# Sixteen merge projections of a hybrid layer: pairs of block products with weight sums and a hand-made order

## The chip, the cores and the metric

The kernel runs on one core of a Trainium2 chip. A core has TensorE (PE, matrix products; its weight loads appear as PEld), VectorE (DVE), ScalarE (ACT), GpSimd (POOL) and SyncE (SP, which issues most DMAs). The metric is device time in microseconds (us), median of several runs. One execution is also profiled; its times are those of the profile's rows.

## What is computed

One layer over 640 tokens (128 of a prompt, 512 of a sample) of width 1024, in fp32. A long convolution branch and a neighbourhood attention branch each give a gated 1024-wide result (here yh and ya). What matters for the change is how they are merged:

```python
p_h = (y_h * silu(g_h)) @ w_bh          # yh . w_bh
p_a = (y_a * silu(g_a)) @ w_ba          # ya . w_ba
m_h, m_a = split(sigmoid(m), 2)         # m: a projection of the layer's input h
out = (m_h * p_h + m_a * p_a) @ w_out
x_new = layer_norm(ALPHA * x + gate * out)
```

## The kernel before

Everything is kept transposed: 128 channels of a tile on the partitions, 640 tokens along the free axis, so 1024 channels are eight tiles (NK = 8). A product of fp32 accuracy is made of three passes in a faster 32-bit format: a value x is split into a high part xh (ACT copies it into that format) and a low part xl = x - xh (DVE), and x.w is taken as wh.xh + wh.xl + wl.xh. `split` (L97) does this; `wtile` (L130) loads a 128x1024 weight tile into a `raw` buffer (two of them) on SP's queue and splits it into `wh` and `wl`. With `eng == "dma"` ACT writes -w instead and a GpSimd DMA (L143) adds the weight onto it.

`proj` (L171) is one projection: an output tile of 128 channels by 640 tokens in a two-bank PSUM tile, by `accumulate` (L161): for each of 8 k tiles three passes of two matmuls of 320 tokens, 48 matmuls. In the profile all of them have the line L166.

The stages are: prologue, convolution, attention (until about 682 us), then the merge:

- `mix_a(n)` (L979) projects h for the gate of the attention branch, tanh on ACT. Two of them come first. The gates of the convolution branch (`mix_h`, L932) were projected during attention.
- The loop at L990: for each n of 8, `proj(T_BH + n, yhH, yhL)`: yh . w_bh. yh is split into yhH (eight 640-token tiles) and yhL. L993 multiplies the result by the gate. Beside it ya is split (yaH, yaL), and `next(side)` runs one of eight gate calls (`gate_rows` L970, `ada` L231: a weight `gate` into a raw buffer, 16 small matmuls).
- The loop at L1018: for each n `mix_a(n + 2)`, then `proj(T_BA + n, yaH, yaL)`: ya . w_ba, gate (L1023), addition of the convolution branch's part (L1024), split into mH and mL, which reuse the tiles of yhH and yhL. After the fifth `gate_bias` (L1002) makes gbc, the gate row of the last addition, by broadcast matmuls.
- L1036: the eight out weights are loaded and split into buffers that are free by then (the tiles of hH and hL among them, which hold h until the last mix_a).
- `out_tile` (L1052) makes one of five out tiles (128 tokens by 1024) of 48 matmuls of 512, `norm_tile` (L1073) gates it, adds x and normalizes, on DVE.

In this stage the order on each engine comes from a scheduler, as far as the waits allow; in the attention PE's order is written by hand.

Of the kernel before, what the change touches and what calls it, by code (L numbers as in the profile page):

```python
# [15 lines left out]
D = 1024  # L16
LP = 128
LS = 512
NK = 8
# [26 lines left out]
def tile_hyena_natten_step(ctx: ExitStack, tc: tile.TileContext, a, o):  # L46
# [57 lines left out]

    out = {"yh": {}}

    def load_pack(i):
# [10 lines left out]

    hH = hp.tile([P, NK, NT], F32R, tag="hH", name="hH")
    hL = hp.tile([P, NK, NT], F32R, tag="hL", name="hL")  # L120
    st = const.tile([P, NK, 32], F32, tag="st", name="st")
# [48 lines left out]

    def proj(i, xh=None, xl=None, eng=None):  # L171
        if i in banks:
            return banks.pop(i)
        w = wtile(i, eng)
        ps = bank(i)
        for k in range(NK):
            accumulate(ps, w, k, xh[k] if xh else hH[:, k], xl[k] if xl else hL[:, k])
            if k < NK - 1:
                yield
        return ps  # L180
# [60 lines left out]
    def prologue():  # L241
# [7 lines left out]
        def work(items, ps):  # L249
            for item in items.split():  # L250
                if item[0] == "w":
                    for _ in range(int(item[1:])):
                        nc.tensor.matmul(ps[:, 256:], hid[:, :P], hid[:, :256], start=True, stop=True, skip_group_check=True)  # L253
                else:
                    i, j = int(item[0]), int(item[1])
                    accumulate(banks[i], early[i], j, hH[:, j], hL[:, j], lead=(0, 1, 2) if j < 1 else (0, 2, 1))

# [18 lines left out]
        for k in range(NK):  # L276
# [32 lines left out]
            for c, s0, n in ((0, PC, LP), (1, SC, LS)):  # L309
                cs = slice(s0, s0 + n)  # L310
                nc.vector.tensor_scalar(hx[:, cs], xt[:, cs], mod[:, 1, c : c + 1], mod[:, 0, c : c + 1], op0=ALU.mult, op1=ALU.add)
                nc.scalar.activation(hH[:, k, cs], xt[:, cs], AF.Identity, scale=mod[:, 1, c : c + 1], bias=mod[:, 0, c : c + 1])  # L312
            nc.vector.tensor_tensor(hL[:, k], hx[:], f(hH[:, k]), op=ALU.subtract)  # L313
            if k == 0:
# [336 lines left out]
    yh, ident = out["yh"], out["ident"]  # L651

# [53 lines left out]
    def values(m):  # L706
# [5 lines left out]
        def passes(k):  # L712
            wh, wl = w[k // 4][0][k % 4], w[k // 4][1][k % 4]
            return ((hH, wh, k == 0, False), (hL, wh, False, False), (hH, wl, False, k == NK - 1))

        for half in range(2):
            ks = range(4 * half, 4 * half + 4)
            for k in ks:
                for x, wk, first, last in passes(k):
                    for t in range(4):  # L720
                        nc.tensor.matmul(  # L721
                            ps[:, t // 2, t % 2 * 256 : t % 2 * 256 + 256], x[:, k, P * t : P * t + P], wk,
                            start=first and t % 2 == 0, stop=last, skip_group_check=True,
                        )
                yield
            if half:
                nc.scalar.activation(v[:, :1024], ps[:].rearrange("p a b -> p (a b)"), AF.Copy)
            else:
                pe = ps_mm.tile([P, 2, 512], F32, tag="mm", name=f"ve{m}")[:, 0]
            for k in ks:  # L730
                for x, wk, first, last in passes(k):
                    nc.tensor.matmul(pe[:, :256], x[:, k, P * 4 :], wk, start=first, stop=last, skip_group_check=True)  # L732
            yield
# [14 lines left out]

    tail = ctx.enter_context(ExitStack())
    ac = ctx.enter_context(ExitStack())  # L750
    ya, tms, edges, biases = [], [], {}, {}

    def attention_setup():
        nonlocal at, mask
        hy.close()
        yap = out["yap"] = tail.enter_context(tc.tile_pool(name="yap", bufs=1, side="right"))
        ya.extend(row(yap, "ya", f"ya{j}", bufs=NK) for j in range(NK))
        at = ac.enter_context(tc.tile_pool(name="at", bufs=1, side="right"))
# [107 lines left out]

    def gated(j, cols, o_):
        nc.vector.tensor_tensor(ya[j][:, cols], out[f"sg{j}"][:, cols], o_, op=ALU.mult)

# [17 lines left out]
    def tiled(i):  # L887
# [39 lines left out]
    def gate_a(j):  # L927
        out[f"sg{j}"] = sg = at.tile([P, NT], F32, tag="sg", bufs=2, name=f"sg{j}") if j else row(yhp, "yh", "sg0")
        yield from gate_tile(T_GA + j, sg[:])
        yield  # L930

    def mix_h():  # L932
        homes = ((0, "q"), (0, "k"), (0, "v"), (), (0, "ql"), (0, "kl"), (1, "q"), (1, "ql"))
        for n in range(NK):
            th = slot(*homes[n], f"mh{n}") if homes[n] else th
            th, pair = (pair[:, NT:], None) if n == 3 else (th[:, :NT], th)
            ps = (yield from proj(T_MH + n))[2]
            nc.scalar.activation(two(th), ps[:, :, :HALF], AF.Tanh, scale=0.5)
            out[f"mh{n}"] = th
            yield  # L940
# [20 lines left out]

    mp = tail.enter_context(tc.tile_pool(name="mp", bufs=1, side="right"))
    lp = left.enter_context(tc.tile_pool(name="lp", bufs=1))
    gpart = slot(1, "v", "gpart")[:, :D]
    yhH = [row(lp, "yhH", f"yhH{n}", F32R, NK) for n in range(NK)]
    yhL = []
    yaH = [row(mp, "yaH", f"yaH{n}", F32R, NK) for n in range(NK)]
    yaL = []

# [9 lines left out]
    def mix_a(n):  # L979
        ps = now(proj(T_MA + n))[2]  # L980
        th = mp.tile([P, NT], F32, tag="th", bufs=3, name=f"mta{n}")
        nc.scalar.activation(two(th[:]), ps[:, :, :HALF], AF.Tanh, scale=0.5)
        return th

    side = gate_rows()
    mtas = [mix_a(0), mix_a(1)]
    for n in range(NK):
        yhL.append(row(yhp, "yh", f"yhL{n}", F32R))
        split(yhH[n][:], yhL[n][:], yh[n][:])
    for n in range(NK):  # L990
        th = out[f"mh{n}"]
        ps = now(proj(T_BH + n, yhH, yhL))[2]
        nc.vector.scalar_tensor_tensor(two(th), two(th), 1.0, ps[:, :, :HALF], op0=ALU.add, op1=ALU.mult)  # L993
        yaL.append(row(out["yap"], "ya", f"yaL{n}", F32R, NK)[:] if n else slot(1, "kl", "yaL0", F32R)[:, :NT])
        split(yaH[n][:], yaL[n], ya[n][:])
        next(side, None)
    mH, mL = yhH, yhL
    gbc = lp.tile([P, 2, D], F32, tag="gbc", name="gbc")
    eps = lp.tile([P, 1], F32, tag="eps", name="eps")
    nc.gpsimd.memset(eps[:], LN_EPS)  # L1000

    def gate_bias():  # L1002
        selr = lp.tile([P, 2], F32R, tag="selr", name="selr")
# [3 lines left out]
        gt = out["slots_r"].tile([P, 2, 384], F32R, tag="k", name="gt")  # L1007
        for c0, n in ((0, 384), (384, 384), (768, 256)):
# [8 lines left out]

    for n in range(NK):  # L1018
        th = mtas.pop(0)
        if n + 2 < NK:  # L1020
            mtas.append(mix_a(n + 2))
        ps = now(proj(T_BA + n, yaH, yaL))[2]
        nc.vector.scalar_tensor_tensor(two(th[:]), two(th[:]), 1.0, ps[:, :, :HALF], op0=ALU.add, op1=ALU.mult)  # L1023
        nc.vector.tensor_tensor(th[:], th[:], out[f"mh{n}"], op=ALU.add)  # L1024
        split(mH[n][:], mL[n][:], th[:])
        next(side, None)
        if n == 4:
            gate_bias()

    wo = []  # L1030
    woh = lp.tile([P, D], F32R, tag="woh", name="woh")
    wol = wp.tile([P, D], F32R, tag="wl", bufs=3, name="wol0")
    wohH = hp.tile([P, 5, D], F32R, tag="hH", name="wohH")
    wolH = hp.tile([P, 5, D], F32R, tag="hL", name="wolH")
    for k in range(NK):
        raw = wp.tile([P, D], F32, tag="raw", name=f"wo{k}")  # L1036
        load_to(raw[:], a["wall"][T_WO + k])
        if k == 0:
            wo.append((woh[:], wol[:]))
        elif k < 6:  # L1040
            wo.append((wohH[:, k - 1], wolH[:, k - 1]))
        else:
            wh = wp.tile([P, D], F32R, tag="wh", name=f"woh{k}")
            wl = wp.tile([P, D], F32R, tag="wl", bufs=3, name=f"wol{k}")
            wo.append((wh[:], wl[:]))
        split(*wo[k], raw[:])


    tail.close()
    fin = ctx.enter_context(tc.tile_pool(name="fin", bufs=1, side="right"))  # L1050
    bc = fin.tile([P, 2, D], F32, tag="bc", name="bc")
    def out_tile(t, split_cols):  # L1052
# [188 lines left out]
```

## Time and profile before

| | |
|---|---|
| median of 3 runs | 925.84 us (925.32 to 926.7) |
| the profiled run | 925.7 us |
| its span | 923.9 us |
| merge and out projection | from about 682 us on |
| last matmul | ends at 915.6 us |
| DVE, ACT, POOL busy | 53%, 41%, 16% of the span |

In a row of a group stand: line, engine, operation, output <- inputs, shape, count; then busy time in all and mean ns of one; then the idle time of its engine just ahead of it and what ended that. A row of the DMA list has the size of one transfer and the median time from issue to landing. A row of the chain of waits in order of time has start, length, engine, line and count of the instructions in that piece.

### The profile page before, as it was taken

The page shows a single profiled execution, that of the slowest core. Times are in us where ns is not written, and L with a number is a line of the kernel's source. Part 1 is how long each engine was busy: PE and PEld are TensorE (multiplying, and loading weights), DVE is VectorE, ACT ScalarE, POOL GpSimd, SP SyncE. Part 2 cuts the span into 40 slices and gives each one's busy share as a digit, 9 for nine tenths or more (in the row PEclk, how much of TensorE's full clock was granted, in tenths as well). Part 3 has the DMA queues.
Part 4 walks back from the last instruction along what each step waited for, and adds up shares of the span by engine and source line. Part 5 has one row for each costly group of instructions (what it writes and reads, how often), then busy time and mean ns, then how long its engine had stood idle before and what let it go on. Part 6 is the DMA issues. An engine that isn't in the chain of part 4 may idle for free.

```text
span 923.9 us, 16758 instructions
## 1 busy us (share of the span) xinstructions
PE 910.2 (99%) x6856; PEld 877.4 (95%) x6856; DVE 486.4 (53%) x948; ACT 380.4 (41%) x776; POOL 146.2 (16%) x188
## 2 busy tenths in 40 slices
PE   8999999999999999999999999999999999999996
PEld 7899999999999999999999999999999999999885
DVE  4776775693796676445352533432261223335676
ACT  4485455554545334255454544444261112223200
POOL 0011010110010000474454543331000000000000
PEclk9999999999999999999999999999999999999998
DMA  8966664655465113242222221212123343224631
GB/s 320 380 161 135 128 149 98 137 133 123 100 141 126 50 49 85 86 122 67 71 68 69 67 70 58 72 49 70 48 69 113 120 146 99 72 69 116 205 114 69
DMA packets 36553, 102.13 MB, mean 111 GB/s; under 512 B 4316, under 2 KB 13020, under 8 KB 36477
## 3 DMA queue, kind: packets, MB, share of 16 engines
q1 hardware_dynamic: 32300, 86.35, 28.9%
q0 software_dynamic: 4032, 14.68, 9.8%
q8 instruction: 54, 0.88, 0.4%
q14 instruction: 23, 0.18, 0.1%
q10 hardware_dynamic: 144, 0.03, 0.0%
HBM read 97.38 MB, written 3.67 MB: 109 GB/s over the span
## 4 chain that ended last, share of the span: by engine, by line
PE 95%; DVE 2%; ACT 2%; issue 1%; POOL 0%; POOLq 0%
PE mm L166 65%; PE out L1065 6%; PE v L721 5%; PE s L788 2%; PE s L831 2%; PE pt L824 2%; PE ve L732 1%; PE adaT L236 1%; PE adaT L253 1%; PE yb L151 1%; PE yb L153 1%; PE yb L152 1%; PE gate L236 0%; PE fl L384 0%; PE fl L385 0%
## 5 line engine op out<-in xcount | busy, mean ns | idle before, releaser
L166 PE MATMUL mm<-hH,wh 128*128 128x320 f32 x1120 | 263.3, 313 | 0.9 <-ACT hH L312 0.6
L166 PE MATMUL mm<-hH,wl 128*128 128x320 f32 x1120 | 259.7, 310 | 0.4 <-DVE wl L99 0.4
L166 PE MATMUL mm<-hL,wh 128*128 128x320 f32 x1120 | 259.1, 310 | 0.0
L99 DVE TENSOR_TENSOR wl<-raw,wh 128x1024 fp32r<-128x1024 f32 x66 | 81.6, 1237 | 231.9 <-ACT wh L98 231.7
L166 PEld LDWEIGHTS mm<-hH,wh 128*128 128x128 f32 x1120 | 186.7, 188 | 6.2 <-issue 4.2
L166 PEld LDWEIGHTS mm<-hH,wl 128*128 128x128 f32 x1120 | 188.0, 188 | 1.4 <-DVE wl L99 1.1
L166 PEld LDWEIGHTS mm<-hL,wh 128*128 128x128 f32 x1120 | 188.2, 188 | 1.1 <-DVE hL L313 0.5
L98 ACT ACTIVATE wh<-raw 128x1024 fp32r<-128x1024 f32 x66 | 69.8, 1059 | 216.8 <-PE mm L166 95.9
L143 POOL DMA_DIRECT2D wl<-wall x28 | 24.3, 869 | 264.0 <-ACT wl L142 208.8
L144 ACT ACTIVATE wh<-raw 128x1024 fp32r<-128x1024 f32 x28 | 29.7, 1060 | 42.9 <-PE mm L166 42.7
L808 POOL TENSOR_SCALAR p<-p,sm 128x384 f32<-128x384 f32 x32 | 42.1, 1326 | 27.7 <-DVE sm L807 27.7
L1095 POOL TENSOR_TENSOR r<-r,bc 128x64 f32<-128x64 f32 x1 | 0.3, 320 | 249.7 <-ACT r L1094 249.7
L808 POOL TENSOR_SCALAR edge<-edge,sm 128x320 f32<-128x320 f32 x32 | 35.5, 1121 | 0.0
L474 DVE SCALAR_TENSOR_TENSOR x<-zs,pack,x 128x641 f32<-128x641 f32 x32 | 28.3, 884 | 12.1 <-ACT x L472 12.0
L826 ACT ACTIVATE pts<-pt 128x384 f32<-128x384 f32 x64 | 26.2, 502 | 11.0 <-PE pt L824 11.0
L142 ACT ACTIVATE wl<-raw 128x1024 fp32r<-128x1024 f32 x28 | 30.0, 1071 | 0.0
L166 PE MATMUL mm<-yhH,wh 128*128 128x320 f32 x128 | 29.9, 315 | 0.0
L166 PE MATMUL mm<-yaH,wh 128*128 128x320 f32 x128 | 29.2, 309 | 0.0
L166 PE MATMUL mm<-yhL,wh 128*128 128x320 f32 x128 | 29.2, 309 | 0.0
L166 PE MATMUL mm<-yaH,wl 128*128 128x320 f32 x128 | 29.2, 309 | 0.0
L166 PE MATMUL mm<-yaL,wh 128*128 128x320 f32 x128 | 29.2, 309 | 0.0
L166 PE MATMUL mm<-yhH,wl 128*128 128x320 f32 x128 | 29.2, 309 | 0.0
(330 smaller groups left out, 1677.7 us busy)
## 6 DMA issues: line engine op xcount, KB each, us to landing
raw<-wall SPq DMA_DIRECT2D x96, 512.0 KB, 3.6
wl<-wall POOLq DMA_DIRECT2D x28, 512.0 KB, 5.8
ada<-wada SPq DMA_DIRECT2D x16, 512.0 KB, 8.1
gate<-wada SPq DMA_DIRECT2D x8, 512.0 KB, 3.7
wo<-wall SPq DMA_DIRECT2D x8, 512.0 KB, 3.7
xt<-xT SPq DMA_DIRECT2D x8, 320.0 KB, 8.1
dec<-decay SPq DMA_DIRECT2D x20, 128.0 KB, 3.5
x<-xB SPq DMA_DIRECT2D x5, 512.0 KB, 3.8
```

Of the source, the lines that this page charges most:

```text
L98: hi = nc.scalar.activation(dst_h, src, AF.Copy)
L99: return hi, (eng or nc.vector).tensor_tensor(dst_l, src, f(dst_h), op=ALU.subtract)
L142: nc.scalar.activation(wl, raw[:], AF.Copy, scale=-1.0)
L143: nc.gpsimd.dma_start(wl, a["wall"][i], accum_op=ALU.add)
L144: nc.scalar.activation(wh, raw[:], AF.Copy)
L166: nc.tensor.matmul(ps[hf][:, :HALF], wt[k], x[:, hf * HALF : (hf + 1) * HALF], start=(i == 0 and k == 0), stop=(i == lead[2] and k == NK - ...
L474: nc.vector.scalar_tensor_tensor(d, zs[:, c : c + NG], convw[:, i, c : c + 1], d, op0=ALU.mult, op1=ALU.add)
L721: nc.tensor.matmul(ps[:, t // 2, t % 2 * 256 : t % 2 * 256 + 256], x[:, k, P * t : P * t + P], wk, start=first and t % 2 == 0, stop=last, ...
L788: nc.tensor.matmul(dst[h], x[rows(h), qs], y[rows(h), ks], start=i == 0, stop=i == 2, skip_group_check=True)
L808: nc.gpsimd.tensor_scalar_mul(pv, pv, sm[:, 2:3])
L826: nc.scalar.activation(ptS[:], pt[:, :384], AF.Copy)
L1065: ins = nc.tensor.matmul(dst, m[k][:, c0 : c0 + P], w[:, c : c + n], start=(first and k == 0), stop=(last and k == NK - 1), skip_group_che ...
```

## The change

Both branches' projections are taken two at a time. A pair is 256 output channels by 640 tokens; with the 1024 input channels cut in two halves of 512 (4 k tiles), the two output tiles and the two token halves of 320, it is a 2 x 2 by 2 x 2 block product. Seven of the eight pairs are done by seven block products instead of eight (Winograd's form), each of 12 matmuls (4 k tiles, 3 passes, 320 tokens); the first BA pair (`PLAIN = 4`) stays plain, in four steps of 24 matmuls.

- The weight sums s3 = a11 - a21, s2 = s3 - a22, s1 = a21 + a22, s4 = a12 + s2 (128x512, DVE) are made for a pair ahead (`SUMS`), from weights loaded a pair ahead (`pair_raws`: even pairs into the two `raw` buffers, odd ones into two of a new pool). `prep(g + 5)` splits the 128x512 weight of the product five steps on; low halves of plain blocks, of s1 and partly of s4 come by an accumulating GpSimd DMA (`halves` with `dma`).
- The token blocks (4 k tiles by 320 tokens, 1280 elements a partition) are read back from DRAM, where yh and ya are now stored as they are made; their sums t1 to t4 are made in place on DVE and split.
- `post` combines the products: u_, w_ and c_ on DVE (the first copy on ACT), then the gates. `merged` adds the convolution branch's part by GpSimd DMAs (the last pair on DVE), `merged_split` splits the result a pair later.
- All eight `mix_a` come first, with the eight gate calls between them. hH and hL become four half tiles, reused for blocks and out weights. Out weights 0, 1, 2 are loaded within the merge, 3 to 7 after the last product. `gate_bias` comes after the merge, in a new pool.
- In the merge the order on PE, DVE and ACT is the program's.

The core of the diff:

```diff
     def gate_conv(n):
             gapped_product(out["yh"][n], out[f"u{n // 2}"][n % 2])
+            nc.sync.dma_start(yh_d[n], out["yh"][n][:])
...
             prompt_values(j, spare.pop(0))
+            nc.sync.dma_start(ya_d[j], ya[j][:])
...
+    def halves(hi, lo, r, dma=None):
+        if dma is None:
+            split(hi, lo, r)
+        else:
+            nc.scalar.activation(lo, r, AF.Copy, scale=-1.0)
+            nc.gpsimd.dma_start(lo, dma, accum_op=ALU.add)
+            nc.scalar.activation(hi, r, AF.Copy)
+    def pair_raws(p):
+        pool, tag, bufs = (wp, "raw", 2) if p % 2 == 0 else (mg, "wa", 2)
+        ts = [pool.tile([P, D], F32, tag=tag, bufs=bufs, name=f"w{pairs[p] + i}") for i in range(2)]
+        for i, t in enumerate(ts):
+            load_to(t[:], a["wall"][pairs[p] + i])
+        wr[p] = [t[:, 512 * h : 512 * h + 512] for t in ts for h in range(2)]
+    SUMS = {-6: "s3", -5: "s2", -4: "s1", -3: "s4"}
+    def prep(g):
...
+        if p == PLAIN:
+            r, dma = wr[p][j], full[j] if j % 2 else None
+        elif j in (0, 4, 5):
+            i = {0: 0, 4: 1, 5: 3}[j]
+            r, dma = wr[p][i], full[i]
+        else:
+            r = ws[p, {1: "s2", 2: "s3", 3: "s1", 6: "s4"}[j]]
+            dma = r if j == 3 or (p > PLAIN and j == 6) else None
+        tag = ("wx", "wh", "wl", "wl", "wh", "wl")[g % 6]
...
+        halves(t[:, 0], t[:, 1], r, dma)
+    def product(g, xb):
...
+            if j == 0:
+                ps_[p] = dict(zip("xy", banks_of(g, 0)[1:]))
+            if j == 2:
+                ps_[p].update(zip("vz", banks_of(g, 2)[1:]))
+            dsts = [(ps_[p]["xyvzxvz"[j]], xb(("b11", "t2", "t3", "t1", "b21", "t4", "b22")[j]))]
+            fresh, done = j < 4, True
+        for k in range(4):
+            wh, wl = (w[:, i, P * k : P * k + P] for i in range(2))
+            for i, (wk, x) in enumerate(((wh, 0), (wh, 1), (wl, 0))):
+                for dst, b in dsts:
+                    nc.tensor.matmul(
+                        dst, wk, b[x][:, k], start=fresh and k == 0 and i == 0,
+                        stop=done and k == 3 and i == 2, skip_group_check=True,
+                    )
+    def post(g):
...
+        if j == 0:
+            nc.scalar.activation(u_, d["x"], AF.Copy)
+        elif j == 1:
+            plus(u_, d["y"], u_)
+        elif j == 2:
+            plus(w_, d["v"], u_)
+        elif j == 3:
+            plus(w_, d["z"], w_)
+            gate(th1, 1, w_)
+        elif j == 4:
+            gate(th0, 0, d["x"])
+        elif j == 5:
+            plus(c_, d["v"], u_)
+            gate(th1, 0, c_)
+        else:
+            plus(c_, d["z"], u_)
+            gate(th0, 1, c_)
...
+    for n in range(1, NK):
+        mtas.append(mix_a(n))
+        next(side)
+        if n == 1:
+            yh_raws()
+            yh_block("b11", 0, 0)
+        if n == 3:
+            r = [rs["y", i] for i in range(4)]
+            minus(r[0], r[1], r[0])
+            minus(r[1], r[2], r[1])
+            minus(r[2], r[0], r[2])
+            yh_block("t2", 2, 1)
+        if n == 4:
+            yh_block("t3", 1, 2)
+            yh_block("t1", 0, 3)
...
+    at_step(0, 0, lambda: yh_block("t4", 3, 5))
+    at_step(0, 1, lambda: yh_block("b22", 4, 6))
+    at_step(1, 0, ya_raws)
+    at_step(1, 4, lambda: ya_block("b11", 1, 7))
+    at_step(3, 1, lambda: ya_block("b12", 2, 0))
+    at_step(3, 2, lambda: ya_block("b21", 0, 1, True))
+    at_step(3, 3, lambda: ya_block("b22", 3, 2))
...
+    at_step(4, 3, lambda: ya_block("t4", 0, 6, True))
+    for p in (4, 5, 6):
+        at_step(p + 1, 1, lambda p=p: merged(p))
+        at_step(p + 1, 5, lambda p=p: merged_split(p))
+    at_step(5, 3, lambda: out_weight(0))
+    at_step(7, 2, lambda: out_weight(1))
+    at_step(7, 5, lambda: out_weight(2))
+    pair_raws(0)
+    pair_raws(1)
+    for name in ("s3", "s2", "s1", "s4"):
+        pair_sum(0, name)
+    yh_block("b21", 3, 4)
+    yh_t4()
+    yh_b22()
+    for g in range(5):
+        prep(g)
+    with tc.manual_schedule(engines={mybir.EngineType.PE, mybir.EngineType.DVE, mybir.EngineType.Activation}):
+        for g, (p, j) in enumerate(kinds):
+            product(g, lambda name: (yx if p < 4 else ax)[name])
+            if g:
+                post(g - 1)
+            if j == 1 and p < 6:
+                pair_raws(p + 2)
+            for q in range(1, 8):
+                if q != PLAIN and g - first[q] in SUMS:
+                    pair_sum(q, SUMS[g - first[q]])
+            prep(g + 5)
+            for fn in extra.get(g, ()):
+                fn()
+        post(len(kinds) - 1)
+        merged(7, False)
+        merged_split(7)
+        for k in range(3, NK):
+            out_weight(k)
...
+    gate_bias()
```

In this listing `kinds` counts the 53 products (seven a pair, four in the plain one), `first[p]` is the first of pair p, and `at_step(p, j, ...)` puts work behind product j of pair p. In the built order DVE and ACT take t4's split ahead of the split of product 1's weight. The load of w81 (second weight tile of pair 0) goes into the raw buffer that the last gate weight held, and SP issues the four yh blocks, w82 and w83 ahead of the weight of the second mix_a.

More of the change, by code (lines that the diff above doesn't have):

```diff
@@ L980, in mix_a @@
         ps = now(proj(T_MA + n))[2]
-        th = mp.tile([P, NT], F32, tag="th", bufs=3, name=f"mta{n}")
+        th = row(yhp, "yh", f"mta{n}")
         nc.scalar.activation(two(th[:]), ps[:, :, :HALF], AF.Tanh, scale=0.5)
-        return th
-    side = gate_rows()
[L986 to L1000, printed above, removed]
+        return th[:]
+    def minus(dst, p, q):
+        nc.vector.tensor_tensor(dst, p, q, op=ALU.subtract)
+    def plus(dst, p, q):
+        nc.vector.tensor_tensor(dst, p, q, op=ALU.add)
+    def halves(hi, lo, r, dma=None):
[5 more added lines that the diff above has]
+            nc.scalar.activation(hi, r, AF.Copy)
```

208 lines of the change are left out of this document (151 added, 57 removed).

## The prediction

> **What bounds the kernel now.** I read the page first (span, engine shares, chain), then the chain in order of time for the merge, then the groups of instructions there, one row for each shape.
>
> ```profile
> span 923.9 us, 16758 instructions
> ...
> PE 910.2 (99%) x6856; PEld 877.4 (95%) x6856; DVE 486.4 (53%) x948; ACT 380.4 (41%) x776; POOL 146.2 (16%) x188
> ...
> PEclk9999999999999999999999999999999999999998
> ...
> PE 95%; DVE 2%; ACT 2%; issue 1%; POOL 0%; POOLq 0%
> PE mm L166 65%; PE out L1065 6%; PE v L721 5%; PE s L788 2%; PE s L831 2%; PE pt L824 2%; PE ve L732 1%; PE adaT L236 1%; PE adaT L253 1%; PE yb L151 1%; PE yb L153 1%; PE yb L152 1%; PE gate L236 0%; PE fl L384 0%; PE fl L385 0%
> ```
>
> TensorE (PE) is busy for 99% of the span, its granted clock is full, and it is 95% of the chain. A matmul fewer is thus time won, and anything that lets PE wait is time lost at once. The profiled run took 925.7 us, 1.8 around its span; the median of the runs is 925.84, so I sum from 925.7 and move nothing.
>
> ```profile
> 703.92 0.57 PE gate L236 x16
> 704.50 7.23 PE mm L166 x48
> ...
> 759.14 70.62 PE mm L166 x480
> ...
> 859.78 55.84 PE out L1065 x264
> ```
>
> The merge on the chain: one projection is 48 matmuls; the 480 of ten projections take 70.62 us, 0.147 us each. A gate call is 0.57, the out projection follows without a gap.
>
> ```profile
> L166 PE MATMUL mm<-yhH,wh 128*128 128x320 f32 x128 | 29.9, 315 | 0.0
> ...
> L99 DVE TENSOR_TENSOR wl<-raw,wh 128x1024 fp32r<-128x1024 f32 x24 | 29.4, 1225 | 68.3 <-ACT wh L98 68.3
> ...
> L98 ACT ACTIVATE wh<-raw 128x1024 fp32r<-128x1024 f32 x23 | 24.4, 1060 | 114.1 <-PE mm L166 61.2 <-DMA raw<-wall 52.1 <-ACT mh L938 0.9
> ...
> L1024 DVE TENSOR_TENSOR mta<-mta,mh 128x640 f32<-128x640 f32 x7 | 5.7, 820 | 0.0
> ...
> L98 ACT ACTIVATE yhH<-mta 128x640 fp32r<-128x640 f32 x7 | 5.2, 737 | 11.4 <-DVE mta L1024 11.4
> ...
> L977 ACT ACTIVATE gpart<-gate 128x512 f32<-128x512 f32 x2 | 1.2, 599 | 4.0 <-PE gate L236 4.0
> ```
>
> The projections' group (128 matmuls, six such groups in BH and BA, 768 in all) has no idle time before it. DVE waits only for ACT, and ACT for freed buffers and loads: both have room.
>
> ```profile
> 780.00:796.00 16.00, 16.00 (x111) 16.00 (x110) 5.38 (x6) 5.11 (x6) 0.00 (x0) 1.00 0.20 66
> ...
> 876.00:892.00 16.00, 16.00 (x71) 12.97 (x70) 12.84 (x25) 1.87 (x3) 0.00 (x0) 1.00 0.37 132
> ```
>
> Columns: stretch, length, then busy time of PE, PEld, DVE, ACT, POOL, clock, DMA share, GB/s. During BA DVE works 5.4 of 16 us and ACT 5.1; in the out projection 71 matmuls fill 16 us, 0.225 each, with DVE at 12.8.
>
> **Part 1: what is removed.** 16 projections are 16 x 48 = 768 matmuls. Seven pairs by seven products of 12 are 588, and the plain pair is 96: 684. So 84 x 0.147 = **-12.4 us**. A product lasts 12 x 0.147 = 1.76 us, a pair 12.35.
>
> **Part 2: what is added to DVE and ACT.** From 820 ns at 640 elements and 1225 at 1024, DVE costs 1.05 ns an element: 0.69 us for 512, 0.48 for 320, 1.49 for 1280 (estimates from these two rows). ACT from 737 and 1060: 0.60 (its own row, 599) for 512, 0.47 for 320, 1.28 for 1280. A Winograd pair asks of DVE four sums (2.7), three low halves (2.1) and nine combinations of 320 (4.4): 9.2 of 12.35 us. It asks of ACT eleven copies (6.6) and u_ (0.5): 7.1. On average both fit, so throughput is not the bound; the order is. All three queues are now fixed, so a wait in one holds what is queued behind it.
>
> **Part 3: the start of pair 0.** The load of w81, the pair's second weight tile, takes the raw buffer of the last gate weight. It can be issued only after that gate's matmuls, which are the last PE work before product 0. Call that moment S.
>
> ```profile
> 703.85 0.64 PE L236 MATMUL gate<-gate,st 128*32 128x128 f32 x16
> ...
> 704.56 0.33 SPq L63 DMA_DIRECT2D raw<-wall  x1
> ...
> 708.05 1.06 ACT L98 ACTIVATE wh<-raw 128x1024 fp32r<-128x1024 f32 x1 [9.78 <-DMA raw<-wall]
> ```
>
> The same hand-over exists in before: gate matmuls end at 704.49, the load is issued at 704.56, ACT starts at 708.05, 3.6 us after. There a whole projection covers it. Here product 1 needs the split of s2 = s3 - a22, and s3 needs w81. DVE does s3 by S + 4.35, s1 by 5.0, s2 by 5.6. ACT has ahead of the high half of s2: the high half of s3 (0.6), two copies for s1 (1.2), two for a22 (1.2), the 1280-wide high half of token sum t4 (1.28); from S + 4.4 these end at 8.7, then wb1's high half at 9.3. DVE, in order, has t4's low half (waits for ACT's 8.7, ends 10.2) and the next pair's s3 (10.9) ahead of wb1's low half, which ends at about S + 11.5. Product 0 ends at S + 1.8; product 1's first two matmuls run at 9.3, the third waits. Stall 11.5 - 1.8 - 0.3 = **9.4**, and products 4 and 5 of that pair wait for u_ and w_, queued on ACT and DVE behind the catching up, **1.5**. Behind this wait stands everything: PE's order is fixed. Lower bound of the stall: the load alone and three steps (s3, s2, high half), S + 3.6 + 0.7 + 0.7 + 0.6 - 1.8 = 3.8. Upper: with the slowest weight landing below (8.3 instead of 3.6), 14.
>
> **Part 4: waits inside the later pairs.** PSUM tiles are shared by two products (v with z, x with y), so product 5, which adds onto v, waits until the addition of z to w_ has read the tile. Product 3 gives z one product (1.76) ahead. On DVE two additions (0.97), s1 (0.69) and a low half (0.69) come after it: 2.35. Some 0.3 to 0.6 is left over; I take 0.4 in each of pairs 1, 2 and 6: **1.2**. Pair 3 has three blocks of 1280 of ya besides: DVE 9.2 + 2 x 1.49 = 12.2 and ACT 7.1 + 4 x 1.28 = 12.2 of 12.35, all slack gone, with a low half of 1.49 ahead of the addition of z in its turn: by walking the queues **4.3**. Pair 5: the low half of token sum t4 comes by a GpSimd DMA, queued behind other accumulating DMAs, and the split of the first out weight stands ahead of the same addition: **2.7**. Bounds for the three: nothing (they have 3 us of slack each on average) and twice as much.
>
> ```profile
> L143 POOL DMA_DIRECT2D wl<-wall x28 | 24.3, 869 | 264.0 <-ACT wl L142 208.8
> ...
> raw<-wall SPq DMA_DIRECT2D x96, 512.0 KB, 3.6
> wl<-wall POOLq DMA_DIRECT2D x28, 512.0 KB, 5.8
> ...
> DMA to landing us min/median/max: 5.4/5.8/8.3
> ```
>
> POOL takes 0.87 to issue one accumulating DMA, and it lands after 5.4 to 8.3 us. The low halves prepared five steps ahead have 5 x 1.76 = 8.8 us, less ACT's negated copy and its wait: the median fits, the slowest doesn't. I take the median, since half-sized tiles carry 256 KB, and cost these at nothing while products run at 1.76; what is late next are the two low halves of j = 4 and 5, at 2 to 3 us each if the slowest landing holds. The gate bias matmuls, moved into the end of the merge, wait for memory held until the last block's DMA: **1.4** (0 to 3).
>
> **Part 5: mix_a.** All eight come first. SP issues four token blocks of 640 KB and two weights, 3.7 MB, ahead of the weight of the second projection.
>
> ```profile
> GB/s 320 380 161 135 128 149 98 137 133 123 100 141 126 50 49 85 86 122 67 71 68 69 67 70 58 72 49 70 48 69 113 120 146 99 72 69 116 205 114 69
> ```
>
> At 380 GB/s, the best slice, that is 9.7 us in which a raw tile must also pass, with 7 us of products beside each; two later loads wait on DVE's 1280-wide sums. I take **2.0**, between nothing and 7. The stores of yh and ya themselves lie in stretches at 50 to 140 GB/s and cost nothing; without that cover they would delay a weight by 1 us.
>
> **Part 6: the end.** Five of eight out weights are split only after the last product (before split them beside BA).
>
> ```profile
> wo<-wall SPq DMA_DIRECT2D x8, 512.0 KB, 3.7
> ...
> bc<-rows SPq DMA_DIRECT2D x2, 512.0 KB, 5.6
> b<-rows SPq DMA_DIRECT2D x1, 512.0 KB, 3.3
> ```
>
> One turn of a raw buffer is 3.7 + 1.06 + 1.23 = 6.0; five weights on two buffers are three turns, to about T + 18 after the merge's end T. PE covers that with the first parts of two out tiles, 96 x 0.225 + gate bias = 23 us of work. The bias load (3.3) waits for a buffer, and the gbc products end near T + 21.6 on a DVE that also splits; then the first tile's 512-wide steps must free PSUM, so that the third tile starts at about T + 26.3: **3.4** (0 to 6).
>
> **Part 7: the clock after a stall.**
>
> ```profile
> 915.00:916.00 1.00, 0.60 (x6) 0.40 (x4) 0.36 (x1) 0.00 (x0) 0.00 (x0) 1.00 0.00 0
> ...
> 917.00:918.00 1.00, 0.00 (x0) 0.00 (x0) 0.91 (x3) 0.29 (x1) 0.00 (x0) 1.00 0.00 0
> 918.00:919.00 1.00, 0.00 (x0) 0.00 (x0) 0.96 (x4) 0.00 (x0) 0.00 (x0) 0.55 0.00 0
> ```
>
> PE's last matmul ends at 915.6; the clock is full up to 918 and then halves: 2.4 us of idleness suffice. So a stall of 9.4 ends at half clock. How long it lasts after PE resumes no row shows; I take as long as the fall, 2.5 us, in which half is lost: **1.3** (0 to 5, if it holds for three stalls).
> The Trainium skill, "TensorE: Matmul & The Clock Gate", section "Part 1: The HAM clock gate", says that the clock halves after an idle window of about 3.4 us and returns after about as long a busy one; the fall here agrees in kind (2.4 us), and no run here shows the return. By that page's figure the loss would be 1.7 for each such stall, an estimate.
>
> **Sum.** -12.4 + 9.4 + 1.5 + 1.2 + 4.3 + 2.7 + 1.4 + 2.0 + 3.4 + 1.3 = **+14.8**: 925.7 + 14.8 = **940.5 us**.
>
> **Rivals.**
> - *Stalls as worked out*, give or take a third: 933 to 947. Chance 0.54. For it: waits taken one by one from the fixed orders. Against it: durations are estimates from other widths.
> - *The clock falls in three stalls, or transfers collide*: the start, pair 3 and pair 5 each exceed 2.4 us. Three losses of 1.3 to 2.5 (half clock for once or twice the time of the fall) instead of one, or the slowest landing, 8.3, for two low halves in three pairs (+6): 943 to 952. Chance 0.19. The skill's page, with a gate that returns only after a busy window, speaks for the first half of it; no run here shows it.
> - *Only start and end*: the later pairs catch up in their slack, mix_a hides its loads: -12.4 + 9.4 + 3.4 = +0.4, and with the rest at its low end up to +3: 926 to 929. Chance 0.11, split about evenly at 927.7.
> - *Faster*: the start is covered. Place: product 1 of pair 0. If the split of s2 is ready within about 2 us of product 0's end (w81's load issued earlier than I read, or the copies ahead of it quicker), the 9.4, 1.5 and the clock's 1.3 go, and the pairs run in their slack: -12.4 + 2.0 + 3.4 = -7: 918.7, at best 913.3. For it: DVE needs 9.2 of 12.35; against it: SP's order puts w81's load behind the gate's matmuls, and the quoted hand-over took 3.6 us. It is on this side only while all waits add up to less than 12.4. Chance 0.12.
> - *Too few matmuls go*: excluded; the counts are in the program, and its PE order holds them. The rest, 0.04, lies above 952.
>
> A difference under 0.2% (1.9 us) cannot be told from none here. Faster 0.12, within 0.05, slower 0.83. The range 919 to 951 leaves out the best case and the far end.
>
> **What would show it.** In the profile after: an idle of 8 to 10 us on PE in the second product of the first pair, ended by DVE's low half of that block; PE share near 97%; windows of pairs 1, 2 and 6 near 12.8 us with PE over 95%, pair 3 with 4 us idle ended by DVE or ACT; DVE over 75% busy in the merge; the third out tile waiting for DVE; a clock under 1.00 in the window after the first stall. Wrong would be: no idle before product 1 (then look at where w81's load stands), or large idle ended by POOL's DMAs in every pair (then the landing times are the cost, and the time is above 950).

## The result and the profile after

The changed kernel takes 962.9 us (median of 4 runs) against 925.9 of the kernel before: ratio 1.04, interval 1.0382 to 1.0418. The forecast was 940.5, in a range of 919 to 951: slower was right, the size was not. 14.8 us of loss were forecast, 37 came.

The page of the changed kernel:

```profile
span 961.9 us, 16941 instructions
...
PE 913.2 (95%) x6772; PEld 874.1 (91%) x6772; DVE 525.5 (55%) x1027; ACT 425.3 (44%) x855; POOL 183.3 (19%) x230
...
PEclk9999999999999999999999999999999799978998
...
q1 hardware_dynamic: 39356, 97.49, 31.2%
q0 software_dynamic: 10080, 27.27, 17.1%
...
PE 76%; DVE 7%; DMA 6%; issue 6%; ACT 3%; POOL 1%; POOLq 0%; SPq 0%; DVEq 0%; ACTq 0%
```

84 matmuls are gone (6856 to 6772), as the change says. Yet PE's busy time has risen from 910.2 to 913.2: some of the rest ran slower, and the row of the clock, full before until the last slice, has holes in its last fifth. PE is 76% of the chain instead of 95%; DVE, DMA, ACT and issue have come in. What PE waited for, in us, times and the longest:

```profile
PE sp L1106 <- DVE tu L1004: 6.5, 7, 3.0
PE gb L1285 <- ACT selr L1275: 6.3, 1, 6.3
PE sp L1106 <- ACT wb L98: 6.0, 1, 6.0
PE out L1304 <- DVE r L1320: 4.0, 1, 4.0
PE sp L1106 <- DMA a_t<-ya: 4.0, 1, 4.0
PE sp L1106 <- DMA wb<-wall: 2.8, 3, 1.7
...
PE sp L1106 <- DVE wb L99: 1.3, 1, 1.3
PE sp L1106 <- DMA wb<-s: 1.2, 1, 1.2
```

These are 28 us in the merge and 4 in the out projection. In the first pair (timeline of PE: start, length, count, in brackets the idle time ahead and what ended it; neighbours are joined, so 24 matmuls are the last product of a pair and the first of the next):

```profile
746.08 0.56 PE L1106 MATMUL sp<-y_b,wb 128*128 128x320 f32 x2
748.35 1.73 PE L1106 MATMUL sp<-y_b,wb 128*128 128x320 f32 x10 [1.71 <-DMA wb<-wall]
756.10 0.90 PE L1106 MATMUL sp<-y_t,wb 128*128 128x320 f32 x2 [6.02 <-ACT wb L98]
758.31 7.67 PE L1106 MATMUL sp<-y_t,wb 128*128 128x320 f32 x34 [1.31 <-DVE wb L99]
765.82 1.92 PE L1106 MATMUL sp<-y_b,wb 128*128 128x320 f32 x12
768.16 2.03 PE L1106 MATMUL sp<-y_t,wb 128*128 128x320 f32 x12 [0.42 <-DVE tu L1004]
770.03 3.69 PE L1106 MATMUL sp<-y_b,wb 128*128 128x320 f32 x24
773.55 5.44 PE L1106 MATMUL sp<-y_t,wb 128*128 128x320 f32 x36
```

S is 746.08. Product 1 starts at 756.10 and goes on at 758.31, S + 12.2. The queues run as part 3 walked them: DVE has s3 only after the weight's landing, ACT takes t4's high half (y_t) ahead of that of product 1's weight, and DVE has t4's low half and the next pair's s3 ahead of that weight's low half:

```profile
750.85 0.69 DVE L1001 TENSOR_TENSOR s<-w,w 128x512 f32<-128x512 f32 x1 [2.40 <-DMA w<-wall]
754.27 1.25 ACT L98 ACTIVATE y_t<-yh 128x1280 fp32r<-128x1280 f32 x1
755.43 0.61 ACT L98 ACTIVATE wb<-s 128x512 fp32r<-128x512 f32 x1
755.56 1.49 DVE L99 TENSOR_TENSOR y_t<-yh,y_t 128x1280 fp32r<-128x1280 f32 x1 [1.61 <-ACT y_t L98]
756.97 0.68 DVE L1001 TENSOR_TENSOR s<-w,w 128x512 f32<-128x512 f32 x1
757.57 0.69 DVE L99 TENSOR_TENSOR wb<-s,wb 128x512 fp32r<-128x512 f32 x1
```

From 758.31 on 34 matmuls take 7.5 us, 0.22 each, while those at 773.55 take 0.147 (36 until 778.83): behind the wait stands half clock. The windows of one us (busy PE, PEld, DVE, ACT, POOL, then clock, DMA share, GB/s):

```profile
752.00:753.00 1.00, 0.00 (x0) 0.00 (x0) 1.00 (x3) 1.00 (x3) 0.00 (x0) 1.00 0.63 232
753.00:754.00 1.00, 0.00 (x0) 0.00 (x0) 0.95 (x2) 1.00 (x3) 0.87 (x1) 0.73 0.02 8
754.00:755.00 1.00, 0.00 (x0) 0.00 (x0) 0.00 (x0) 1.00 (x2) 0.85 (x1) 0.50 0.52 92
...
762.00:763.00 1.00, 1.00 (x5) 1.00 (x5) 0.63 (x1) 1.00 (x2) 0.00 (x0) 0.50 1.04 279
...
764.00:765.00 1.00, 1.00 (x9) 1.00 (x8) 1.00 (x2) 0.53 (x2) 0.69 (x1) 1.00 0.25 91
```

PE stops at 750.1, the clock halves at 753.5, and it is full again at 763.7, 5.4 us after PE went on. Five stalls of the run do this. The times with PE at work at half clock are 758.3 to 763.7, 811.5 to 814.9, 846.4 to 852.4, 882.8 to 886.5 and 917.3 to 920.7: 22.0 us, so about 11.0 are lost.

The largest stalls that the forecast had small, product 5 of pair 5 and the gate bias products in pair 7 (timeline of PE):

```profile
840.80 0.41 PE L1106 MATMUL sp<-a_t,wb 128*128 128x320 f32 x1 [1.10 <-DVE tu L1004]
845.18 0.63 PE L1106 MATMUL sp<-a_t,wb 128*128 128x320 f32 x1 [3.97 <-DMA a_t<-ya]
846.42 3.04 PE L1106 MATMUL sp<-a_t,wb 128*128 128x320 f32 x10 [0.60 <-DMA wb<-wall]
...
882.76 1.01 PE L1285 MATMUL gb<-gt,selr 128*128 128x384 f32 x2 [6.26 <-ACT selr L1275]
883.57 0.84 PE L1286 MATMUL gb<-gt,selr 128*128 128x384 f32 x2
884.21 3.00 PE L1106 MATMUL sp<-a_t,wb 128*128 128x320 f32 x12
887.05 1.93 PE L1106 MATMUL sp<-a_b,wb 128*128 128x320 f32 x12
888.81 0.51 PE L1285 MATMUL gb<-gt,selr 128*128 128x384 f32 x2
```

Both go back to accumulating GpSimd DMAs. For the second, ACT's rows: selr, which the product needs, stands behind the split of mH, and that waits for an addition by DMA, then selr itself for the last block's DMA, which holds its memory.

```profile
880.92 0.74 ACT L98 ACTIVATE mH<-mta 128x640 fp32r<-128x640 f32 x1 [5.62 <-DMA mta<-mh]
882.51 0.20 ACT L1275 ACTIVATE selr<-pack 128x2 fp32r<-128x2 f32 x1 [0.85 <-DMA wb<-s]
```

The DMAs of 826 to 850 us (queue, kind: packets, MB, share of 16 engines' time; q0 has the accumulating DMAs of GpSimd, q1 the plain loads; then issues: size, median us to landing):

```profile
q0 software_dynamic: 1296, 2.88, 67.7%
q1 hardware_dynamic: 432, 1.57, 19.0%
...
wb<-wall POOLq DMA_DIRECT2D x3, 256.0 KB, 11.4
...
a_t<-ya POOLq DMA_DIRECT2D x1, 640.0 KB, 11.8
```

The low half of t4 lands after 11.8 us, and weights behind it after 11.4. The DMA engines are full: 87% of their 24 us go to 4.45 MB. By these two rows accumulating traffic passes at 2.88 MB in 16.2 us, 177 GB/s, plain loads at 1.57 MB in 4.6, 344 GB/s.

By pairs (starts read off the timeline, a pair of 84 matmuls at 0.147 is 12.35 us), the loss over full rate:

| | forecast | measured |
|---|---|---|
| pair 0 (746.08 to 771.8) | 12.2 with the clock | 13.4 |
| pairs 1 and 2 | 0.8 | 1.4 |
| pair 3 (797.9 to 815.9) | 4.3 | 5.7 |
| the plain pair | 0 | 0 |
| pair 5 (830.0 to 852.4) | 2.7 | 10.1 |
| pair 6 | 0.4 | 2.4 |
| pair 7 (867.2 to 888.8), gate bias | 1.4 | 9.2 |
| mix_a | 2.0 | 2.4 |
| out projection | 3.4 | 5.8 |
| matmuls | -12.4 | -12.4 |
| sum | +14.8 | +38.0 (spans) |

The last measured entry, 5.8, is the rest to the difference of the spans; 4.0 of it is the wait for r (above) and 1.7 the half clock behind. Pair 7's 9.2 hold the first four gate bias products, 1.45 us at half clock.

### The profile page after: what moved, and what is told of

Same layout as the page of the kernel before. It is cut to its first block, busy times and chain, and to the rows that moved or that the text cites. A ratio compares the mean times of both kernels' runs of the same rounds, so it can differ in the third digit from the quotient of the medians.

```text
span 961.9 us, 16941 instructions
## 1 busy us (share of the span) xinstructions
PE 913.2 (95%) x6772; PEld 874.1 (91%) x6772; DVE 525.5 (55%) x1027; ACT 425.3 (44%) x855; POOL 183.3 (19%) x230
## 3 DMA queue, kind: packets, MB, share of 16 engines
q0 software_dynamic: 10080, 27.27, 17.1%
## 4 chain that ended last, share of the span: by engine, by line
PE 76%; DVE 7%; DMA 6%; issue 6%; ACT 3%; POOL 1%; POOLq 0%; SPq 0%; DVEq 0%; ACTq 0%
PE mm L176 48%; PE sp L1106 4%; PE v L732 4%; DMA raw<-wall 2%; PE s L839 2%; PE s L796 2%; PE pt L832 2%; PE out L1304 1%; DMA wb<-wall 1%; DMA wb<-s 1%; PE ve L743 1%; PE adaT L246 1%; ACT wh L98 1%; DVE wl L99 1%; POOL wb L1011 1%
## 5 line engine op out<-in xcount | busy, mean ns | idle before, releaser
L99 DVE TENSOR_TENSOR wl<-raw,wh 128x1024 fp32r<-128x1024 f32 x50 | 61.6, 1234 | 210.0 <-ACT wh L98 209.9
L98 ACT ACTIVATE wh<-raw 128x1024 fp32r<-128x1024 f32 x50 | 52.9, 1060 | 143.1 <-issue 56.6
L1304 PE MATMUL out<-wo,mH 128*128 128x512 f32 (+1 forms) x176 | 47.5, 384 | 4.0 <-DVE r L1320 4.0
L1011 POOL DMA_DIRECT2D wb<-wall x23 | 20.3, 882 | 151.9 <-ACT wb L1012 104.2
L154 ACT ACTIVATE wh<-raw 128x1024 fp32r<-128x1024 f32 x28 | 29.6, 1059 | 42.9 <-PE mm L176 42.7
L1106 PE MATMUL sp<-y_t,wb 128*128 128x320 f32 x192 | 34.0, 337 | 11.6 <-ACT wb L98 6.0
L1106 PEld LDWEIGHTS sp<-y_t,wb 128*128 128x128 f32 x192 | 31.7, 209 | 13.3 <-ACT wb L98 6.3
L1304 PEld LDWEIGHTS out<-wo,mH 128*128 128x128 f32 x176 | 32.6, 193 | 11.3 <-DVE r L1320 4.2
L1106 PE MATMUL sp<-a_b,wb 128*128 128x320 f32 x204 | 33.3, 319 | 1.8 <-DMA wb<-s 1.2
L484 DVE SCALAR_TENSOR_TENSOR x<-zs,pack,x 128x641 f32<-128x641 f32 x32 | 28.2, 882 | 12.2 <-ACT x L482 12.1
L1106 PEld LDWEIGHTS sp<-a_b,wb 128*128 128x128 f32 x204 | 31.8, 197 | 2.5 <-DMA wb<-s 1.4
L1106 PE MATMUL sp<-a_t,wb 128*128 128x320 f32 x144 | 25.7, 335 | 6.2 <-DMA a_t<-ya 4.0
L834 ACT ACTIVATE pts<-pt 128x384 f32<-128x384 f32 x64 | 26.2, 501 | 10.9 <-PE pt L832 10.9
```

The lines of the kernel that those rows point to most:

```text
L98: hi = nc.scalar.activation(dst_h, src, AF.Copy)
L99: return hi, (eng or nc.vector).tensor_tensor(dst_l, src, f(dst_h), op=ALU.subtract)
L154: nc.scalar.activation(wh, raw[:], AF.Copy)
L484: nc.vector.scalar_tensor_tensor(d, zs[:, c : c + NG], convw[:, i, c : c + 1], d, op0=ALU.mult, op1=ALU.add)
L834: nc.scalar.activation(ptS[:], pt[:, :384], AF.Copy)
L1011: nc.gpsimd.dma_start(lo, dma, accum_op=ALU.add)
```

## The experiments

The theory after the result (A): the loss is named waits of PE, each with its own cause, and half clock behind each long one. Rivals: (B) the transfers are the bound, so a wait that is removed comes back elsewhere; (C) DVE and ACT have no room, so order does not matter.

**Pair 0's weights early** (e1).

```diff
-        pool, tag, bufs = (wp, "raw", 2) if p % 2 == 0 else (mg, "wa", 2)
+        pool, tag, bufs = (wp, "raw", 2) if p % 2 == 1 else (mg, "wa", 2)
```

> Pair 0's two weights go into the new pool's buffers (loaded before the second mix_a), pair 1's into the raw buffers. Theory A (named waits, and half clock after each): the 9 us of idle of products 0 and 1 and the 2.5 us of half clock behind them go; pair 0 takes 13 to 14 us instead of 25.7, and the time falls by 10 to 12, to 951 to 953. Rival B (transfers are the bound): the same bytes still have to pass, the waits reappear in pair 1 or in mix_a, time down by less than 4. Rival C (DVE and ACT behind): product 1 still waits for its low half, down by less than 4.

Measured 945.8, 17.1 less. Pair 0 takes 14.5 us instead of 25.7: 11.2 of it. 4.6 more come from pairs 6 and 7, which the forecast had not seen. With pair 7's weights in the raw buffers, the second and third out weight are loaded in pair 7 (issued at 854.8 and 855.9) and no longer at the start of pair 6 (852.0 and 853.8), and pair 6's wait of 1.2 for a low half of s4 is gone; the scheduler puts the gate bias products behind the last product, where selr is ready. That these two are the causes is read off the order and not tested. B and C are wrong for the start: nothing comes back.

**selr ahead of the merge** (e2), in a pool of its own:

```diff
+    selr = const.tile([P, 2], F32R, tag="selr", name="selr")
+    nc.scalar.activation(selr[:], sel, AF.Copy, scale=0.25)
...
-        selr = fin.tile([P, 2], F32R, tag="selr", name="selr")
-        nc.scalar.activation(selr[:], sel, AF.Copy, scale=0.25)
```

> The small tile selr is made ahead of the merge in a pool of its own, so that the gate bias product ahead of product 51 doesn't wait for the pool's memory, which the last block's accumulating DMA holds. Theory A: 6.3 us of idle and about 1.8 of half clock go, and the last product waits a little for that same DMA: down 5 to 8, to 955 to 958. Rival B (the late DMA is the bound): product 52 needs the same DMA at most 2 us later, the wait moves there: down by less than 3.

Measured 956.9, 6.0 less. The 6.3 of idle are gone, and 2.6 come back as the last product's own wait for that DMA: mostly A, and B for the part that it named. In the profiled run, 7.4 shorter, pair 7 gives 5.3; 2.7 come from pairs 0, 3 and 5, which the edit does not touch: they have 6.8, 0 and 6.8 us of half clock here against 10.2, 3.4 and 10.2. That part is luck (the last section says why).

**The additions on DVE** (e3) instead of by accumulating DMA:

```diff
-        at_step(p + 1, 1, lambda p=p: merged(p))
+        at_step(p + 1, 1, lambda p=p: merged(p, False))
```

> The six additions of the convolution branch's part (320 KB each) go from accumulating GpSimd DMAs to DVE (0.82 us each). Theory A as put by the queue: a low half that comes by DMA stands behind these 320 KB transfers; without them pair 5's token sum lands 3 to 5 us sooner and pairs 6 and 7 lose their DMA waits (1.2 and most of 6.3): down 8 to 14, to 949 to 955. Rival (landing is slow for every accumulating DMA by itself, 640 KB takes 10 us): down by less than 3, or up by the 4.9 us of DVE work.

Measured 949.1, 13.9 less. The median landing of the low halves of s4 (3 of 256 KB), in the kernel after the change and then here:

```profile
wb<-s POOLq DMA_DIRECT2D x3, 256.0 KB, 10.2
```
```profile
wb<-s POOLq DMA_DIRECT2D x3, 256.0 KB, 4.4
```

The same transfer lands in under half the time once 1.9 MB of accumulating traffic is out of the way: most of its landing time was the queue ahead of it. Pair 7 takes 13.0 us instead of 21.6 and has no wait for selr, pair 6 13.0 instead of 14.7, pair 5 20.2 instead of 22.5.

**Idle matmuls in the long stalls** (e4): products are repeated into an unused PSUM bank.

```diff
+    WARM = {(0, 1): 54, (3, 5): 24, (5, 5): 36, (7, 5): 40}
...
+            if (p, j) in WARM:
+                scrap = aux(f"scrap{g}")
+                for i in range(WARM[p, j]):
+                    nc.tensor.matmul(scrap[:, :HALF], wlast[:, 0, :P], xlast[0][:, 0], start=True, stop=True, skip_group_check=True)
```

> Idle matmuls into an unused PSUM bank (54 ahead of product 1, 24, 36 and 40 ahead of product 5 of pairs 3, 5 and 7) fill most of the four long stalls; the computation is unchanged and 154 matmuls (22.6 us at full clock) are added. Theory A: the waits stay where they are, but TensorE doesn't fall to half clock, so 8 to 9 us of slow products go: 953 to 956. Rival (the slow matmuls behind a stall come from something else, contention for instance, or the dummies delay the products): 960 to 975.

Measured 955.3, 7.6 less, with 154 matmuls more. They take 22.6 us in place of about 22 us of idle, so these waits are about as long as before; what is gone is the slow work behind them. By pairs: 2.3, 1.2 and 3.9 us less in pairs 0, 3 and 5, where 2.7, 1.7 and 3.0 had been lost at half clock; pair 6 is 2.0 longer, its wait for a low half of s4 being 2.4 instead of 1.2. (In this run the gate bias products come behind the last product; the 40 idle matmuls stand in the place of their wait.) Windows of the kernel after the change, then of this one (the clock is the third number from the end):

```profile
750.00:760.00 10.00, 2.67 (x9) 2.19 (x9) 5.79 (x8) 5.51 (x9) 2.60 (x3) 0.67 0.80 185
...
880.00:890.00 10.00, 7.24 (x34) 7.11 (x35) 4.31 (x6) 3.46 (x6) 0.00 (x0) 0.67 0.71 239
```
```profile
740.00:760.00 20.00, 19.16 (x139) 18.23 (x139) 9.59 (x12) 11.31 (x18) 3.51 (x4) 1.00 0.71 169
...
880.00:900.00 20.00, 20.00 (x88) 16.34 (x88) 11.23 (x14) 8.28 (x10) 0.00 (x0) 1.00 0.50 167
```

**The three together** (e5: early, selr, additions on DVE).

> The three edits before together: pair 0's weights early, selr ahead, the additions on DVE. Theory A (each wait is its own cause): the start is worth 12 to 13, the additions 14 with the wait of the gate bias in it: 962.9 - 26 = 937, give or take 3. Rival B (transfers are the bound and waits only move): above 943.

Measured 937.7: 25.3 less, within A's range. The three single gains add up to 37.0, but each of them takes out the wait for selr, and e1 and e3 both the loss of pair 6, so they overlap there. Pair 0's 11.2 and the 13.9 of the additions add up to 25.1: these two are separate causes.

**Order on DVE** (e6), on top of it:

```diff
-                post(g - 1)
+                q, i = kinds[g - 1]
+                if q == PLAIN or i not in (2, 3):
+                    post(g - 1)
+                elif i == 3:
+                    post(g - 2)
+                    post(g - 1)
...
-    at_step(3, 3, lambda: ya_block("b22", 3, 2))
+    at_step(3, 5, lambda: ya_block("b22", 3, 2))
```

> As the run before, and two moves in DVE's order: the addition of v to w_ is done directly ahead of that of z, and the 1280-wide split of ya's block b22 two products later. Theory A: the waits of 0.42 in six pairs and pair 3's 0.7 + 2.95 with 1.5 of half clock behind go: 5 to 8 less than the run before, 929 to 932. Rival C (DVE has no room, the order is beside the point): the same waits under another name, less than 2 us.

Measured 932.9, 4.8 less: just short of A's 5 to 8, and more than C allows. The small waits of pairs 1, 2 and 6 and pair 3's 2.9 are gone; a wait of 1.9 in pair 5 is left.

**The end** (e7), on top of it:

```diff
+        rs["b0"] = wp.tile([P, D], F32, tag="wl", bufs=3, name="b0")
...
+    at_step(7, 3, load_b0)
...
-        for k in range(3, NK):
-            out_weight(k)
...
     gate_bias()
+    for k in range(3, NK):
+        out_weight(k)
```

> As the run before, and at the end: the bias row is loaded during the last pair, and the gate bias comes ahead of the last five out weights' splits. Theory A: the third out tile's wait of 4.0 and 1.5 of half clock go: 923 to 927, about the kernel before. Rival: the out weights come later by as much, the wait moves ahead into the first tiles: no change against the run before.

Measured 927.2, 5.7 less, 0.2 above A's range. The out tile's wait is gone. Ratio to the kernel before: 1.0014 (1.0005 to 1.0023).

**All low halves on DVE** (e8, on top of e6, without the end's change): `halves` ignores `dma`.

> As e6, with every low half in the merge made by DVE, none by accumulating DMAs. DVE's work for a pair rises from 9.2 to about 12 us of 12.35, ACT's falls by 2.4. Theory A: the remaining waits for DMAs (about 4 with their half clock) go, but DVE is late in the pairs with 1280-wide blocks: from 3 faster to 8 slower than e6. Rival B (accumulating DMAs are what costs): 5 or more faster than e6.

Measured 938.4, 5.6 more than that run. The window from 740 to 860 us:

```profile
740.00:860.00 120.00, 108.30 (x717) 104.37 (x716) 104.60 (x162) 51.27 (x78) 0.00 (x0) 0.99 0.30 97
```

DVE is busy for 104.6 of 120 us, the DMA share is 0.30, no wait of the merge is for a DMA any more, and 11.7 us are for DVE. So B isn't the whole: with the transfers gone, the waits are for DVE.

**Four tries at what e7 has left.** Its waits in the merge and the mix:

```profile
PE sp L1106 <- DVE tu L1004: 4.5, 4, 1.9
PE sp L1106 <- DMA wb<-wall: 3.3, 3, 2.1
PE mm L176 <- DVE wl L99: 1.2, 2, 0.9
```

The first, e9, on top of e7 (the run of the end):

```diff
-    at_step(0, 1, lambda: yh_block("b22", 4, 6))
+    at_step(0, 4, lambda: yh_block("b22", 4, 6))
...
-        at_step(p + 1, 1, lambda p=p: merged(p, False))
-        at_step(p + 1, 5, lambda p=p: merged_split(p))
-    at_step(5, 3, lambda: out_weight(0))
+        at_step(p + 1, 5, lambda p=p: merged(p, False))
+        at_step(p + 1, 6, lambda p=p: merged_split(p))
+    at_step(6, 3, lambda: out_weight(0))
```

> As e7, and three moves of work away from the waits left: the split of yh's block b22 three products later in pair 0, the load and split of the first out weight from pair 5 to pair 6, the additions on DVE from product 1 to product 5 of a pair. Theory A: pair 0's waits for u_ and w_ (1.0 + 0.9) and pair 5's (1.9 on DVE, part of 2.1 on a DMA, 3 of half clock behind) go: 4 to 6 less than e7, 921 to 923, faster than the kernel before. Rival C (DVE has no room): less than 2, 925 to 927.

Measured 931.7: 4.6 more than e7, a miss, and worse than the rival had it. Pair 0's wait for w_ shrinks, but its last block is late; pair 5's wait for DVE goes from 1.9 to 0.4, but its DMA wait of 2.1 stays and one of 0.9 is new; the additions in product 5 bring two new waits of 0.45, and the first out tiles wait 1.9 for an out weight.

e10, on top of e9:

```diff
-    at_step(4, 3, lambda: ya_block("t4", 0, 6, True))
+    at_step(4, 3, lambda: ya_block("t4", 0, 6))
```

> As e9, with the low half of ya's t4 (640 KB) made by DVE and not by an accumulating DMA. Theory A: the DMAs queued behind it in pair 5 land 2 to 3 us sooner, and DVE has 1.5 more at the end of the plain pair, where it has room: 0 to 3 less than e9. Rival: DVE is late for pair 5's first posts, up to 2 more than e9.

Measured 929.6, 2.1 less than e9: pair 5 has no DMA wait and no half clock left, and DVE holds the plain pair's bank 1.4 and pair 6 1.1 us.

e11, on top of e7, and e12, the same with the additions on DVE (without the last four lines):

```diff
-    at_step(0, 1, lambda: yh_block("b22", 4, 6))
-    at_step(4, 3, lambda: ya_block("t4", 0, 6, True))
-    at_step(5, 3, lambda: out_weight(0))
+    at_step(0, 2, lambda: yh_block("b22", 4, 6))
+    at_step(5, 1, lambda: ya_block("t4", 0, 6))
+    at_step(6, 1, lambda: out_weight(0))
...
-        at_step(p + 1, 1, lambda p=p: merged(p, False))
+        at_step(p + 1, 1, lambda p=p: merged(p))
...
-                nc.gpsimd.dma_start(mtas[n], out[f"mh{n}"], accum_op=ALU.add)
+                nc.gpsimd.tensor_tensor(mtas[n], mtas[n], out[f"mh{n}"], op=ALU.add)
```

> As e7, with: the six additions by GpSimd's own arithmetic, neither DVE nor DMA; the split of yh's block b22 one product later; the low half of ya's t4 on DVE during pair 5; the first out weight's split in pair 6. Theory A (what is left of e7's loss is pair 5, where DVE's work of the BA pairs exceeds 12.35 us a pair): pair 0's waits shrink by 1, pair 5's 1.9, 2.1 and 3 of half clock go: 920 to 923. Rival: GpSimd's additions are so slow (its 384-wide operations took 1.3 us each in the kernel before) that they hold the DMAs queued behind them: 925 to 929.

Measured 928.6: in the rival's range, but not for its reason. GpSimd takes 1.6 to 2.8 us for an addition (DVE 0.82) and nothing waits long for it (ACT once, 0.7); but the waits for DVE add up to more than in e7:

```profile
PE sp L1106 <- DVE tu L1004: 6.7, 6, 1.8
PE sp L1106 <- DMA wb<-wall: 2.2, 2, 1.4
```

> As e11, with the six additions on DVE as in e7. Theory A: pair 5's DMA waits go, but DVE stays over its 12.35 us in pairs 5 and 6: 922 to 926, 1 to 4 above e11. Rival: DVE's load does not matter, equal to e11.

Measured 930.3. The order of e11 and e12 is as expected, both levels 4 to 9 us above it. The time of the pairs, from start to start:

| us | pair 0 | pair 3 | plain | pair 5 | pair 6 | pair 7 |
|---|---|---|---|---|---|---|
| e7 | 14.9 | 13.3 | 15.0 | 19.2 | 12.3 | 13.8 |
| e9 | 14.7 | 13.3 | 15.0 | 18.1 | 13.9 | 15.0 |
| e10 | 14.7 | 13.3 | 14.8 | 14.1 | 14.6 | 16.6 |
| e11 | 16.1 | 13.3 | 15.2 | 15.0 | 14.8 | 15.3 |
| e12 | 16.1 | 13.3 | 15.2 | 17.0 | 14.5 | 15.6 |

Pair 5 gains up to 5.1 us, and pairs 6, 7 and 0 together lose as much or more: a piece taken out of one queue's way stood in another's. Here C holds, at this level and not at that of the change itself. Against the kernel before, run beside each, the ratios are 1.0014 for e7 and 1.0063, 1.0034, 1.0024 and 1.0054 for e9 to e12; the intervals of e7 and e11 overlap. None of the runs beats the kernel before.

## Why the prediction was wrong in size

- **The gain** was right: 84 matmuls, 12.4 us.
- **The start** (9.4 + 1.5) was right in place and cause, and near in size: product 1 goes on at S + 12.2 (S + 11.5 forecast), and the run with early weights gives 11.2 back in pair 0. Its own waits are 6.0 and 1.3, less than the 9.4, and 0.4 stands for the 1.5; a wait of 1.71 in product 0, for its own low half by DMA, was not foreseen. That the sum of the waits, 9.5 for 10.9, is so near is in part luck.
- **The clock** was the largest error of a single term. Part 7 took one stall, and a return as fast as the fall: 1.3. There were five stalls long enough, and at half clock PE worked for 3.4 to 6.0 us behind each: 11.0. The step that failed is "I take as long as the fall, 2.5 us" for one stall; stalls that the same text had priced at 4.3 and 2.7 were above its own limit of 2.4 and belonged in that sum. The run with idle matmuls shows it: 7.6 back with these waits about as long as before. The Trainium skill, "TensorE: Matmul & The Clock Gate", "Part 1: The HAM clock gate", gives about 3.4 us of idleness for the fall and as much work for the return, in windows that run free. The trace agrees with the windows and their length: the stretches at half clock last 10.2, 3.4, 10.2, 6.8 and 3.4 us. Less than a whole idle window is enough for the fall, though: the stall of pair 3 was 2.95 us.
- **The landing of accumulating DMAs** was costed "at nothing", by the median of the kernel before (5.8), whose 28 such DMAs lie between 49 and 290 us, with the DMA engines at four to six tenths. In pairs 5 to 7 they stand in one queue behind 320 and 640 KB: 11.8 for t4, 10.2 for s4. Pair 5 got 10.1 instead of 2.7 (6.2 of idle, the rest half clock), and taking 1.9 MB of this traffic out gave 13.9 us. The second rival named both this and the clock, with an "or" between them, and ended at 952; both came. The prediction's own sign of this, large idle ended by POOL's DMAs and a time above 950, came true in part, in pairs 5 and 7.
- **The gate bias** was sized 1.4 with an end at 3: it took the landing above (6.3), and 2.9 for four of its products and for half clock behind.
- **Pair 3, the small waits, mix_a and the end** were right within 2.4 us each, all too low.
- **"DVE needs 9.2 of 12.35"**, the argument for the fast rival, fits pairs 1 to 3 (DVE is busy for 9.9, 8.5 and 9.0 us there in e7). The BA pairs carry additions, splits of the result, token blocks and out weights besides: 13.6 us in the plain pair, whose matmuls take 14.1, 12.3 in pair 5, 10.2 and 10.3 in pairs 6 and 7. In the merge of the changed kernel DVE is busy for 60% (85.8 of 142.7 us), not the "over 75%" of the prediction. e8 to e12 fit with DVE's work in the plain pair and pair 5 being the last bound; no run has less of it there with everything else left alone, so this is argued. With the start, the additions, the order and the end mended (e7), the seven-product form saves 12.4 us of PE and gives 14 back: 9 in waits, 2.6 at half clock (826.6 to 833.4 us of e7, with PE at work from 828.2), the rest in small gaps. Which part of the last 9 could still go by another distribution of work is open.

## What to carry to other kernels

When PE is the bound and fewer matmuls are bought with work on other engines, add up that work for the busiest stretch, not for the average one, and walk the fixed queues there. Price every stall of PE above 2 to 3 us twice: once for itself, once for the half clock behind it (1.7 to 3.0 us a stall here). Take the landing time of a DMA from its queue at that moment, with everything issued ahead, not from the median of another stretch.

## What was not expected of the hardware

- The clock changes on a grid. In every run here the changes lie whole multiples of 3.41 us apart; half clock lasts 3.4, 6.8 or 10.2 us (but for the last one, which the end of the run cuts off). So the fall comes 2.4 to 4.4 us after PE stops (912.9 to 917.3 the longest) and the return 3.8 to 6.0 us after it works on (846.4 to 852.4 the longest), by where the stall lies on the grid: pair 3's stall of 2.95 brought 3.4 us of half clock in the changed kernel, where one step of the grid (808.1 to 811.5) had PE busy for 0.21 of it, and none in e2, where it fell into two steps with 0.59 and 0.55.
- How idle a step of that grid must be can be worked out from the matmul records of all 14 runs. A step of 3.41 us with PE busy for less than 0.44 of it was always followed by half clock, one with more than 0.49 never. At half clock, a step with PE busy for 0.82 or less never brought the full clock back, one with 0.84 or more always did.
- Accumulating DMAs take about twice the engine time of plain loads for a byte: 177 against 344 GB/s in the crowded stretch. Over the whole of the kernel before it is the same, by the rows of its queues: 14.68 MB in 9.8% against 86.35 MB in 28.9% of the span, 162 against 323 GB/s. All accumulating DMAs here are issued by GpSimd and all plain loads by another engine, so the runs don't tell which of the two it is.
